# Down-projection weight sums made during the up stage and streamed, in a float32 transformer layer on one core

## The chip, the core and the metric

The kernel runs on one core of a Trainium2 chip. The metric is the device time of one launch in microseconds. Five engines work side by side: TensorE (PE in the profile, PEld its weight loads), VectorE (DVE), ScalarE (ACT), GpSimd (POOL), and SyncE (SP), which here only issues DMAs. Each engine runs its own list of instructions in order and waits on semaphores for the others. TensorE's clock is granted in two levels, 2.4 GHz (1.00 in the profile) and 1.2 GHz (0.5).

## The reference

One layer of a generator over 2048 tokens of width 1024. Only its second half matters here:

```
h2 = modulate(rmsnorm(x, norm2_g), shift, scale)
gate, up = split(h2 @ w_up, 2)               # w_up: 1024 x 5632, so 2816 columns each
gate = depthwise_conv(gate, conv_w, conv_b)  # 3 taps along the tokens
x = x + mod * ((silu(gate) * up) @ w_down)   # w_down: 2816 x 1024
return rmsnorm(x, final_norm_g)              # all float32
```

The 2816 hidden channels are 22 blocks of 128, in two halves of 11.

## The kernel before

The first 1060 us (modulation, first projection, the three head groups and the output projection) are not touched. Then comes the feed-forward part, in two stages.

**Float32 by three matmuls.** Every operand is split by `halves` into a high half (copied by ACT, line 1100) and a low half (a subtraction on DVE or POOL, line 1101; the fifth argument says which). A product of two split operands is three matmuls: high by high, high by low, low by high.

**One level of Winograd's scheme.** Both matrix products are cut in 2 by 2 blocks and done with seven products of block sums in place of eight: B11, T2, T1, T3, B21, T4, B22, numbered 0 to 6 in the names. So the operands are sums of blocks: T1 uses a21+a22 of the weights, T2 that less a11, B22 a12 less that, T3 a11-a21.

**Up stage.** Tokens go in two halves, t = 0 and 1. For each t there are eleven pairs k: one `winograd` for the gate (names `g_k`) and one for the up half (`u_k`), each 84 matmuls of 128x512 on line 1290. DVE empties the PSUM banks x, y, z (lines 1301 to 1312), ACT starts the convolution (line 1341) and DVE does its other two taps (line 1343), POOL makes the sums of the next weights and of the results, and POOL's DMA queue stores the results to DRAM (`actd`). The generator `second_half`, advanced by `step`, prepares the second token half during t = 0. During t = 1 `step` does nothing.

**Down stage.** For each t seven `product`s in the order B11, B21, T2, T1, T3, B22, T4, each of 11 k with 12 matmuls of 128x512 (line 1487) into four PSUM banks (named p, pu or pv). The activations come back from `actd` in tiles `ra` of two k; their halves are `ah`. `w_down` (four blocks, 11.5 MB) is loaded to SBUF once, in pieces, over the first products, and stays. `down_weight` makes the sums for T2, T1, T3 and B22 again for each t, on POOL (names `dw..s`, lines 1447 to 1451), for B22 partly on DVE (1451, 1453), and its halves are `dw..hl` (the digits are t, product and k). POOL also does the low halves of `ra` for B11, B21, T4 and every second one of B22: 72 in all.

After a product, `adds` adds its banks to the residual tile `x1r` (line 1501), squares what is final on ACT (1504), adds up the squares on DVE (1508), and `finish` makes the statistics: one matmul against ones (1513), square root (1519), reciprocal (1520) and eight scalings (1526, 1524), with the stores of the output.

**What sets the order.** The program is written in one stream; a scheduler orders each engine's list by a simulated timeline when it is built, under the limits of the tile pools (a tag with `bufs=n` is a ring of n buffers; a new tile waits for the readers of the one it replaces). Loads go through SP's queue, stores of the up stage through POOL's. On the chip each list is strictly in order.

Of the kernel before, what the change touches and what calls it, by code (L numbers as in the profile page):

```python
# [18 lines left out]
P = 128  # L19
# [14 lines left out]
TB = 512  # L34
# [109 lines left out]
def tile_hybrid_block(ctx: ExitStack, tc: tile.TileContext, a, out):  # L144
# [41 lines left out]
          for p in range(7)]  # L186
    actd = [[dp.tile([P, NP, TB], F32, name=f"actd{t}{p}") for p in range(7)] for t in range(2)]
# [1094 lines left out]
    last_up = [None]  # L1282
# [11 lines left out]
    def winograd(w, c12, c21, c22, use_c11, name, step):  # L1294
# [10 lines left out]
        nc.vector.tensor_tensor(c22, c22, z, op=ALU.add)  # L1305
# [9 lines left out]
    def up_pair(t, k, wg, wu):  # L1315
        nm = f"{t}_{k}"

        def step():
            if t == 0 and k > 0:
                next(sh, None)  # L1320
# [15 lines left out]
        for i, l in ((0, 0), (1, 1), (1, 0), (0, 1)):  # L1336
# [3 lines left out]
            ps = c if t else pp.tile([P, TB], F32, tag="st", bufs=1, name=f"cs{nm}{i}{l}")  # L1340
# [42 lines left out]
    sh = second_half()  # L1383
    for t in range(2):
# [14 lines left out]
    with ExitStack() as down:  # L1399
# [4 lines left out]
        dn, dx, da, dw0, dpad, dwh, dw1, dah, dw2 = (pool(f"dn{i}") for i in range(9))  # L1404
        dpad.tile([P, 2048], F32, name="dpad")
# [3 lines left out]
        CH = ((0, 4), (4, 8), (8, NP))  # L1409
        wq = {}  # L1410

        def wd_tiles(i, j, pool):
            wq[i, j] = [pool.tile([P, b - a_, TB], F32, name=f"wd{i}{j}{a_}") for a_, b in CH]

        def wd_load(i, j, c):
            load(wq[i, j][c], a["w_down"][i, j][:, CH[c][0]:CH[c][1], :])

        def x1_tile(t, l, fo):
            return dx.tile([P, TB], F32, tag="x1", bufs=16, name=f"x1r{t}{l}{fo}")
# [6 lines left out]
        X1_ORDER = [(l, 4 * i + m) for i, l in ((0, 0), (0, 1), (1, 1), (1, 0)) for m in range(4)]  # L1426
        wd_tiles(0, 1, dw0)
        wd_tiles(1, 0, dw0)
        wd_tiles(0, 0, dw1)
        wd_tiles(1, 1, dw2)  # L1430
        x1s = [{lf: x1_tile(0, *lf) for lf in X1_ORDER}, {}]
        for c in range(3):
            wd_load(0, 0, c)
        none = [(lambda: None, ())]
        x1_loads = [(x1_load, (0,) + lf) for lf in X1_ORDER]
        ahead = iter(none * 10 + [(wd_load, (0, 1, 0))] + none * 3
                     + x1_loads[:4] + [(wd_load, (0, 1, 1)), (wd_load, (0, 1, 2))] + x1_loads[4:]
                     + [(wd_load, (1, j, c)) for c in range(3) for j in range(2)])

        def down_weight(p, k, name):  # L1440
            a11, a12, a21, a22 = (wq[i, j][k // 4][:, k % 4, :] for i in range(2) for j in range(2))
            if p in (B11, B21, T4):
                src = {B11: a11, B21: a12, T4: a22}[p]
            else:
                src = dn.tile([P, TB], F32, tag="ws", bufs=3, name=name + "s")
                if p == T3:
                    nc.gpsimd.tensor_tensor(src, a11, a21, op=ALU.subtract)
                else:
                    nc.gpsimd.tensor_tensor(src, a21, a22, op=ALU.add)
                    if p != T1:  # L1450
                        (nc.vector if p == B22 else nc.gpsimd).tensor_tensor(src, src, a11, op=ALU.subtract)
                        if p == B22:
                            nc.vector.tensor_tensor(src, a12, src, op=ALU.subtract)
# [188 lines left out]
```

## Time and profile before

| | |
|---|---|
| median of 3 runs | 2392.19 us (2389.84 to 2395.36) |
| the profiled execution | 2384.91 us, span 2382.9 us |
| PE busy | 2268.9 us, 95% |
| DVE busy | 1818.5 us, 76% |
| POOL busy | 1045.1 us, 44% |
| down stage, first to last matmul | 1903.0 to 2364.7 us |

The profile is one execution. Busy times are sums over the instructions of an engine; a wait of DVE for its operands' port inside an instruction counts as busy. A row of the timeline is one instruction, or several alike in a row (the xN at its end), and the bracket behind it says how long the engine stood idle before it and what released it.

### The profile page before, as it was taken

The numbers are of one execution on the slowest core, as the hardware profiler recorded it, in microseconds if no ns is written. First come the engines' busy times: TensorE is split into PE (matmuls) and PEld (weight loads), VectorE is DVE, ScalarE is ACT, GpSimd is POOL, SyncE is SP. The second block draws the span as 40 slices with busy tenths as digits, with TensorE's granted clock in tenths as the row PEclk, the third lists the DMA queues.
The fourth block names the chain that finished last, engine by engine and source line by source line (L and its number), as shares of the span: only waits on it lengthen the run. The fifth ranks groups of instructions, "written<-read, shape, count | busy, mean of one in ns | idle before, by whom it ended". The sixth has DMA issues, their size and how long they took to land.

```text
span 2382.9 us, 34374 instructions
## 1 busy us (share of the span) xinstructions
PE 2268.9 (95%) x12452; PEld 1890.4 (79%) x12452; DVE 1818.5 (76%) x2503; ACT 1140.8 (48%) x2018; POOL 1045.1 (44%) x982
## 2 busy tenths in 40 slices
PE   7999989999999899999999999999999999989996
PEld 5889768988888688878787887788888887768875
DVE  4786656556785884796899977687787889988997
ACT  4764643357455446554444534344343444344442
POOL 0265312111012122225656665556556477665763
PEclk9999999999999999999999999999999999999998
DMA  9775576657878778643344435433333482245322
GB/s 352 241 243 181 197 238 189 184 171 230 247 223 274 204 211 298 225 160 104 142 162 174 162 130 204 162 103 111 101 107 106 157 334 89 80 150 165 96 81 92
DMA packets 179226, 421.70 MB, mean 177 GB/s; under 512 B 19952, under 2 KB 68976, under 8 KB 177008
## 3 DMA queue, kind: packets, MB, share of 16 engines
q1 hardware_dynamic: 144688, 318.82, 42.5%
q0 software_dynamic: 28320, 94.39, 10.6%
q10 hardware_dynamic: 6048, 6.29, 0.8%
q8 instruction: 98, 1.61, 0.3%
q14 instruction: 72, 0.59, 0.1%
HBM read 311.69 MB, written 107.74 MB: 176 GB/s over the span
## 4 chain that ended last, share of the span: by engine, by line
PE 51%; DVE 21%; DMA 12%; issue 8%; ACT 4%; POOL 3%; SPq 1%; DVEq 0%; ACTq 0%; POOLq 0%
DVE cv L573 3%; PE po L202 3%; PE obank L202 3%; PE pu L1487 2%; PE p L1487 2%; PE pq L202 2%; PE s L202 2%; PE tp L208 2%; DVE ah L1101 2%; PE pk L202 2%; PE tp L202 2%; PE pv L1487 2%; DMA bias_t<-in_bias 1%; DMA kk<-ks 1%; POOL ah L1101 1%
## 5 line engine op out<-in xcount | busy, mean ns | idle before, releaser
L573 DVE SCALAR_TENSOR_TENSOR cv<-hconv,cst,cv 128x512 f32<-128x512 f32 x240 | 214.5, 935 | 10.8 <-ACT cv L567 10.6
L693 DVE CUSTOM_DVE_ANT_0 sb<-s,bias_t 128x544 f32<-128x544 f32 (+3 forms) x128 | 105.1, 821 | 105.7 <-PE s L202 73.8
L696 ACT ACTIVATE sb<-sb,mx 128x544 f32<-128x544 f32 (+3 forms) x128 | 106.3, 831 | 161.5 <-DVE mx L693 158.6
L1101 POOL TENSOR_TENSOR ah<-ra,ah 128x512 fp32r<-128x512 f32 x72 | 110.5, 1548 | 79.0 <-ACT ah L1100 79.0
L1100 ACT ACTIVATE ah<-ra 128x512 fp32r<-128x512 f32 x154 | 95.0, 622 | 93.5 <-PE p L1487 28.6
L202 PE MATMUL s<-kk,qq 128*128 128x256 f32 (+4 forms) x512 | 102.8, 323 | 14.9 <-DVE mx L693 7.5
L202 PEld LDWEIGHTS s<-kk,qq 128*128 128x128 f32 x512 | 88.4, 191 | 34.7 <-DVE mx L693 13.7
L208 PE MATMUL tp<-cst,sb 128*128 128x128 f32 (+2 forms) x672 | 97.9, 276 | 12.9 <-DVE pt L728 9.1
L208 PEld LDWEIGHTS tp<-cst,sb 128*128 128x128 f32 (+2 forms) x672 | 80.0, 139 | 32.4 <-DVE pt L728 10.6
L1345 ACT ACTIVATE c<-c 128x512 f32<-128x512 f32 x88 | 55.4, 630 | 100.8 <-DVE c L1343 100.6
L1343 DVE SCALAR_TENSOR_TENSOR c<-gb,cst,c 128x512 f32<-128x512 f32 x88 | 97.5, 1131 | 1.5 <-ACT c L1341 1.3
L1101 DVE TENSOR_TENSOR ah<-ra,ah 128x512 fp32r<-128x512 f32 x82 | 83.9, 1028 | 12.4 <-ACT ah L1100 12.4
L196 POOL DMA_DIRECT2D x1d<-x x30 | 16.4, 548 | 143.1 <-DVE x L859 109.8
L966 POOL TENSOR_TENSOR adaf<-adaf,adaf 128x1024 f32<-128x1024 f32 x16 | 41.1, 2568 | 84.4 <-ACT adaf L963 84.4
L726 ACT ACTIVATE pt<-tp 128x384 f32<-128x384 f32 (+2 forms) x128 | 61.0, 477 | 35.5 <-PE tp L208 35.1
L728 DVE COPY pt<-tp 128x256 f32<-128x256 f32 (+1 forms) x128 | 57.6, 450 | 23.4 <-PE tp L208 23.0
L963 ACT ACTIVATE adaf<-adaf,silu_c 128x256 f32<-128x256 f32 x128 | 54.2, 497 | 43.8 <-DMA adaf<-in_ada 40.0
L196 POOL DMA_DIRECT2D ks<-k x60 | 33.4, 559 | 78.7 <-ACT k L226 48.6
L196 POOL DMA_DIRECT2D mixd<-att x14 | 7.7, 554 | 134.1 <-DVE att L227 130.2
L196 POOL DMA_DIRECT2D actd<-c x66 | 36.6, 554 | 65.2 <-DVE c L1353 47.9
L202 PE MATMUL obank<-pt,vt 128*64 128x128 f32 (+2 forms) x832 | 58.4, 277 | 0.2 <-DVE pt L728 0.2
L1353 DVE TENSOR_TENSOR c<-c,u 128x512 f32<-128x512 f32 x66 | 52.1, 790 | 0.5
(2411 smaller groups left out, 8015.5 us busy)
## 6 DMA issues: line engine op xcount, KB each, us to landing
ra<-actd SPq DMA_DIRECT2D x70, 512.0 KB
wg<-in_w_up SPq DMA_DIRECT2D x44, 512.0 KB
wu<-in_w_up SPq DMA_DIRECT2D x44, 512.0 KB
actd<-tt POOLq DMA_DIRECT2D x88, 256.0 KB, 2.4
actd<-c POOLq DMA_DIRECT2D x66, 256.0 KB, 2.3
adaf<-in_ada SPq DMA_DIRECT2D x32, 512.0 KB
qq<-qs SPq DMA_DIRECT2D x64, 256.0 KB
adaf<-in_ada SPq DMA_DIRECT2D x8, 1024.0 KB
```

The costliest lines, as they stand in the source:

```text
L196: st_eng[0].dma_start(plain(dst), plain(src))
L202: x = nc.tensor.matmul(*args, **kw)
L208: x = nc.tensor.transpose(*args)
L573: nc.vector.scalar_tensor_tensor(acc[ct], hb[:, ct, k:k + TB], cvw[:, ct, k:k + 1], acc[ct], op0=ALU.mult, op1=ALU.add)
L693: x = nc.vector.tensor_tensor_reduce(out=sb[:, w], in0=s[:, w], in1=bt[:, w], scale=-1.0, scalar=3.0e38, op0=ALU.add, op1=ALU.min, accum_o ...
L696: nc.scalar.activation(sb[:, w], sb[:, w], AF.Exp, bias=mx, scale=-1.0, accum_out=rs[:, cb, j:j + 1])
L726: nc.scalar.activation(dst, src, AF.Copy)
L728: nc.vector.tensor_copy(dst, src)
L1100: nc.scalar.activation(hl[:, 0, :], src, AF.Copy)
L1101: eng.tensor_tensor(hl[:, 1, :], src, hl[:, 0, :].bitcast(F32), op=ALU.subtract)
L1343: nc.vector.scalar_tensor_tensor(to, gb[:, i, o + d:o + d + TB], fcw[:, f, d:d + 1], ps, op0=ALU.mult, op1=ALU.add)
L1487: nc.tensor.matmul(ps[i], w[:, ww, sl], ah[:, aa, :], start=start and k_ == 0 and m == 0, stop=(k_ == NP - 1 and m == 2), skip_group_check ...
```

## The change

1. `down_sums`, a generator advanced by `step` in the pairs k >= 2 of t = 1, loads `w_down` once more, in 22 pieces of 512 KB (ring `sp` of 3), makes the four sums with 4 DVE additions per k (44 in all) in place, and stores them with 22 stores of 512 KB through POOL's queue to two DRAM tensors `sd`.
2. In t = 1 (but not for k = 10) the first convolution tap is written to a PSUM bank, as it was in t = 0 already.
3. In the down stage no sums are made. Each product loads its own weights, two k at a time, from `w_down` or `sd` (tiles `wd`, ring of 4). The ring of `ra` has 3 buffers, before 4; `ah` has two rings of 4, before one of 6. All 32 tiles of the residual are loaded early. POOL does the low halves of the activations for B21 alone (22), DVE all others. The halves of the first six k of the first product are issued after the last addition of c22 of the up stage.
4. The last statistics (t = 1, first half of the tokens) take the last square unsummed, as a second matmul into the same bank, in columns: 8 matmuls of one column, square root and reciprocal on 128x4, 4 matmuls that spread the result, and one ACT copy for POOL; DVE reads it from PSUM.

The matmuls of the products are the same in number, kind and order. Line numbers shift: 1101 becomes 1103, 1304 to 1310 become 1324 to 1330, 1353 becomes 1375, 1501 and 1508 become 1495 and 1504. Over the whole program POOL's tensor_tensor instructions go from 533 to 373 and its DMAs from 328 to 350, DVE's tensor_tensor from 1239 to 1288, and SP's weight loads for the down stage from 12 to 84, beside the 22 of `down_sums`.

```diff
+    sd = [dp.tile([P, NP, 2, TB], F32, name=f"sd{j}") for j in range(2)]
+    def down_sums():
+        yield
+        for k in range(NP):
+            x, y = (fws.tile([P, 2, TB], F32R, tag="sp", bufs=3, name=f"wds{k}{j}").bitcast(F32) for j in range(2))
+            for j, q in ((0, x), (1, y)):
+                with tc.issue_after(last_w[0]):
+                    load(q, a["w_down"][:, j, :, k, :].rearrange("i p c -> p i c"))
+            a11, a21, a12, a22 = x[:, 0, :], x[:, 1, :], y[:, 0, :], y[:, 1, :]
+            nc.vector.tensor_tensor(a22, a21, a22, op=ALU.add)
+            nc.vector.tensor_tensor(a21, a11, a21, op=ALU.subtract)
+            yield
+            nc.vector.tensor_tensor(a11, a22, a11, op=ALU.subtract)
+            nc.vector.tensor_tensor(a12, a12, a11, op=ALU.subtract)
+            for j, q in ((0, x), (1, y)):
+                store(sd[j][:, k], q)
+            yield
...
-            if t == 0 and k > 0:
+            if t and k > 1:
+                next(dw, None)
+            elif not t and k > 0:
                 next(sh, None)
...
-            ps = c if t else pp.tile([P, TB], F32, tag="st", bufs=1, name=f"cs{nm}{i}{l}")
+            ps = c if t and k == NP - 1 else pp.tile([P, TB], F32, tag="st", bufs=1, name=f"cs{nm}{i}{l}")
...
+        DOWN_W = {B11: a["w_down"][0, 0], B21: a["w_down"][0, 1], T4: a["w_down"][1, 1],
+                  T2: sd[0][:, :, 0, :], T3: sd[0][:, :, 1, :], B22: sd[1][:, :, 0, :], T1: sd[1][:, :, 1, :]}
...
-                        at = da.tile([P, 2, TB], F32, tag="ra", bufs=4, name=f"ra{t}{p}{k}")
+                        wt = dwd.tile([P, 2, TB], F32, tag="wd", bufs=4, name=f"wd{t}{p}{k}")
+                        load(wt[:, 0:n, :], DOWN_W[p][:, k:k + n, :])
+                        at = da.tile([P, 2, TB], F32, tag="ra", bufs=3, name=f"ra{t}{p}{k}")
                         last_ra[0] = load(at[:, 0:n, :], actd[t][p][:, k:k + n, :])
...
-                    ah = halves(at[:, k % 2, :], dah, "ahl", 6, f"ah{t}{p}{k}",
-                                nc.gpsimd if p in (B11, B21, T4) and (t or p or k > 3) or p == B22 and k % 2 else nc.vector)
+                    order = tc.issue_after(last_c22[0]) if (t, p) == (0, B11) and k < 6 else nullcontext()
+                    with order:
+                        ah = halves(at[:, k % 2, :], (dah, dai)[k % 2], "ahl", 4, f"ah{t}{p}{k}",
+                                    nc.gpsimd if p == B21 else nc.vector)
+                        wh = halves(wt[:, k % 2, :], dwh, "whl", 6, f"dw{t}{p}{k}", nc.vector)
...
-                    ops.append((k, down_weight(p, k, f"dw{t}{p}{k}"), ah))
+                    ops.append((k, wh, ah))
...
+                if last:
+                    sq = acc[l], acc["last"]
+                    for i in range(4):
+                        for j, x in enumerate(sq):
+                            mm(ps[:, i:i + 1], x[:, i * P:(i + 1) * P], ones_d[:, 0:1], start=j == 0, stop=j == 1)
...
+                    col = cp.tile([P, 4], F32, tag="col", bufs=2, name=f"frs{t}{l}")
+                    nc.scalar.activation(col, ps[:, 0:4], AF.Sqrt, bias=eps)
+                    nc.vector.reciprocal(col, col)
+                    pr = dnp.tile([P, TB], F32, tag="y", name="fmr")
+                    for i in range(4):
+                        mm(pr[:, i * P:(i + 1) * P], col[:, i:i + 1].to_broadcast([P, P]), ident, start=True, stop=True)
+                    r = dn.tile([P, TB], F32, tag="rstd", bufs=1, name="frs")
+                    nc.scalar.activation(r, pr, AF.Copy)
```

How the change moves DVE's list is shown at three places; in a row stand the line, the operation, what is written and what is read. The first is in pair 3 of t = 1, around the drains of the gate's banks (`g1_3y`, `g1_3z`). Before:

```order
L1305 TENSOR_TENSOR gb_10781<-gb_10781,g1_3z_15386 128x512
L1101 TENSOR_TENSOR wu1_3hl3_15501<-wu1_3s2_15486,wu1_3hl3_15501 128x512
L1343 SCALAR_TENSOR_TENSOR c1_300_15513<-gb_10781,cst_75,c1_300_15513 128x512
L1310 TENSOR_TENSOR gb_10781<-g1_3p1_15387,g1_3y_15385 128x512
L1101 TENSOR_TENSOR wu1_3hl4_15504<-wu1_30_15480,wu1_3hl4_15504 128x512
L1343 SCALAR_TENSOR_TENSOR c1_311_15518<-gb_10781,cst_75,c1_311_15518 128x512
```

Now, where `wds40` and `wds41` are the two tiles of `down_sums` for k = 4:

```order
L1325 TENSOR_TENSOR gb_10783<-gb_10783,g1_3z_15416 128x512
L1270 TENSOR_TENSOR wds41_15835<-wds40_15834,wds41_15835 128x512
L1103 TENSOR_TENSOR wu1_3hl3_15541<-wu1_3s2_15526,wu1_3hl3_15541 128x512
L1365 SCALAR_TENSOR_TENSOR cs1_300_15554<-gb_10783,cst_75,cs1_300_15554 128x512
L1271 TENSOR_TENSOR wds40_15834<-wds40_15834 128x512
L1103 TENSOR_TENSOR wg1_4hl0_15714<-wg1_40_15702,wg1_4hl0_15714 128x512
L1273 TENSOR_TENSOR wds40_15834<-wds41_15835,wds40_15834 128x512
L1274 TENSOR_TENSOR wds41_15835<-wds41_15835,wds40_15834 128x512
L1330 TENSOR_TENSOR gb_10783<-g1_3p1_15417,g1_3y_15415 128x512
```

The four additions stand between the last addition of c22 (1325, before 1305) and the drain for c21 (1330, before 1310), where two weight halves and a convolution tap stood; this repeats once per winograd.

The second place is the end of the up stage, DVE's last drains of the winograd `u1_10` and the first halves of the down stage (`dw00..` weights, `ah00..` activations of product B11, t = 0). Before:

```order
L1304 TENSOR_TENSOR u_10780<-u1_10p1_17615,u1_10y_17613 128x512
L1376 TENSOR_TENSOR pc_83<-ue_82,pc_83 128x11
L1101 TENSOR_TENSOR dw000hl_17828<-wd000_17794,dw000hl_17828 128x512
L1305 TENSOR_TENSOR u_10780<-u_10780,u1_10z_17614 128x512
L1101 TENSOR_TENSOR dw001hl_17846<-wd000_17794,dw001hl_17846 128x512
L1101 TENSOR_TENSOR dw002hl_17866<-wd000_17794,dw002hl_17866 128x512
L1353 TENSOR_TENSOR c1_1011_17597<-c1_1011_17597,u_10780 128x512
L1101 TENSOR_TENSOR dw003hl_17884<-wd000_17794,dw003hl_17884 128x512
L1101 TENSOR_TENSOR dw004hl_17904<-wd004_17795,dw004hl_17904 128x512
L1101 TENSOR_TENSOR dw005hl_17923<-wd004_17795,dw005hl_17923 128x512
L1310 TENSOR_TENSOR u_10780<-u1_10p1_17615,u1_10y_17613 128x512
```

Now:

```order
L1325 TENSOR_TENSOR u_10782<-u_10782,u1_10z_17766 128x512
L1103 TENSOR_TENSOR dw000_17987<-wd000_17980,dw000_17987 128x512
...
L1103 TENSOR_TENSOR ah005_18088<-ra004_18066,ah005_18088 128x512
L1103 TENSOR_TENSOR dw005_18091<-wd004_18064,dw005_18091 128x512
L1103 TENSOR_TENSOR ah002_18024<-ra002_18022,ah002_18024 128x512
L1375 TENSOR_TENSOR c1_1011_17749<-c1_1011_17749,u_10782 128x512
L1103 TENSOR_TENSOR ah004_18068<-ra004_18066,ah004_18068 128x512
L1330 TENSOR_TENSOR u_10782<-u1_10p1_17767,u1_10y_17765 128x512
```

Between the addition of c22 (1325) and the next drain (1330) there are now twelve low halves, eleven ahead of the product c1_1011 and one behind it (seven are left out above), where there were five; the weight halves `dw000` that stood ahead of 1305 are behind it.

The third is in the down stage, product B22 of t = 0 (`dw06..`, `ah06..`). Before, with the sums `dw06..s` between the halves:

```order
L1453 TENSOR_TENSOR dw066s_19206<-wd014_17789,dw066s_19206 128x512
L1451 TENSOR_TENSOR dw067s_19228<-dw067s_19228,wd004_17795 128x512
L1451 TENSOR_TENSOR dw068s_19253<-dw068s_19253,wd008_17796 128x512
L1453 TENSOR_TENSOR dw067s_19228<-wd014_17789,dw067s_19228 128x512
L1101 TENSOR_TENSOR dw066hl_19210<-dw066s_19206,dw066hl_19210 128x512
L1453 TENSOR_TENSOR dw068s_19253<-wd018_17790,dw068s_19253 128x512
L1101 TENSOR_TENSOR ah068_19250<-ra068_19247,ah068_19250 128x512
L1101 TENSOR_TENSOR dw067hl_19232<-dw067s_19228,dw067hl_19232 128x512
L1101 TENSOR_TENSOR dw068hl_19257<-dw068s_19253,dw068hl_19257 128x512
L1451 TENSOR_TENSOR dw069s_19263<-dw069s_19263,wd008_17796 128x512
L1453 TENSOR_TENSOR dw069s_19263<-wd018_17790,dw069s_19263 128x512
L1451 TENSOR_TENSOR dw0610s_19276<-dw0610s_19276,wd008_17796 128x512
```

Now:

```order
L1103 TENSOR_TENSOR dw065_19314<-wd064_19288,dw065_19314 128x512
L1103 TENSOR_TENSOR ah066_19334<-ra066_19331,ah066_19334 128x512
L1504 TENSOR_TENSOR sq014_19192<-sq014_19192,sq017_19203 128x512
L1103 TENSOR_TENSOR dw066_19337<-wd066_19329,dw066_19337 128x512
L1103 TENSOR_TENSOR ah068_19375<-ra068_19372,ah068_19375 128x512
L1103 TENSOR_TENSOR dw067_19355<-wd066_19329,dw067_19355 128x512
L1103 TENSOR_TENSOR ah069_19381<-ra068_19372,ah069_19381 128x512
L1103 TENSOR_TENSOR dw068_19378<-wd068_19370,dw068_19378 128x512
L1103 TENSOR_TENSOR ah0610_19392<-ra0610_19389,ah0610_19392 128x512
L1103 TENSOR_TENSOR dw069_19384<-wd068_19370,dw069_19384 128x512
L1103 TENSOR_TENSOR ah051_19494<-ra050_19473,ah051_19494 128x512
L1103 TENSOR_TENSOR dw0610_19395<-wd0610_19387,dw0610_19395 128x512
```

The sums (1451, 1453) are gone, and in their place stand the low halves of the activations with odd k, which POOL made before, each ahead of the weight halves of the k before it.

## Rows read from the trace of the kernel before

**Rows 1.** The page, engines over the whole span: busy us (share) x instructions.

```profile
PE 2268.9 (95%) x12452; PEld 1890.4 (79%) x12452; DVE 1818.5 (76%) x2503; ACT 1140.8 (48%) x2018; POOL 1045.1 (44%) x982
```

**Rows 2.** Windows: from:to, length, busy (instructions) per engine, PEclk, DMA share, GB/s.

```profile
1903.00:2365.00 462.00, 437.76 (x1855) 352.90 (x1853) 421.68 (x411) 194.52 (x365) 293.08 (x191) 0.97 0.41 138
2079.00:2086.00 7.00, 6.05 (x14) 4.79 (x15) 6.96 (x8) 1.87 (x4) 4.80 (x3) 0.51 0.12 49
```

**Rows 3.** Timeline of PE, down stage: start, duration, engine, line, operation, count.

```profile
1903.01 2.88 PE L1487 MATMUL p<-ah,dw000hl 128*128 128x512 f32 x12
1905.73 2.88 PE L1487 MATMUL p<-ah,dw001hl 128*128 128x512 f32 x12
...
2364.05 0.84 PE L1487 MATMUL pu<-ah,dw1510hl 128*128 128x512 f32 x3
```

**Rows 4.** Waits of PE, down stage: waiter, releaser, us in total, times, longest.

```profile
PE fms L1513 <- DVE sq L1508: 7.4, 2, 5.4
PE pv L1487 <- ACT dw066hl L1100: 1.7, 1, 1.7
...
PE pv L1487 <- DVE ah L1101: 0.3, 1, 0.3
```

**Rows 5.** Groups by line, down stage: count, busy us, mean ns, idle before.

```profile
L1101 POOL TENSOR_TENSOR ah<-ra,ah 128x512 fp32r<-128x512 f32 x72 | 110.5, 1548 | 79.0 <-ACT ah L1100 79.0
L1101 DVE TENSOR_TENSOR ah<-ra,ah 128x512 fp32r<-128x512 f32 x82 | 83.9, 1028 | 12.4 <-ACT ah L1100 12.4
```

**Rows 6.** Line 1101, down stage: ns shortest/median/longest, first and last start.

```profile
L1101 DVE TENSOR_TENSOR ah<-ra,ah x82: 673/684/1785, 1902.7 to 2321.2; 128x512 fp32r<-128x512 f32 x82
```

**Rows 7.** Windows: six pairs of t = 0, then three of t = 1.

```profile
1130.00:1370.00 240.00, 231.54 (x1003) 189.90 (x1003) 215.98 (x262) 108.19 (x181) 153.39 (x184) 0.99 0.46 161
1591.00:1705.00 114.00, 114.00 (x505) 94.41 (x504) 90.37 (x111) 46.89 (x77) 66.09 (x66) 1.00 0.31 105
```

**Rows 8.** Waits of PE, up stage of t = 0.

```profile
PE g_2y L1290 <- DVE gb L1304: 3.4, 1, 3.4
```

**Rows 9.** Groups, DVE's convolution taps: in t = 1, then in t = 0.

```profile
L1343 DVE SCALAR_TENSOR_TENSOR c<-gb,cst,c 128x512 f32<-128x512 f32 x80 | 91.7, 1170 | 1.5 <-ACT c L1341 1.3
...
L1343 DVE SCALAR_TENSOR_TENSOR cs<-gb,cst,cs 128x512 f32<-128x512 f32 x37 | 27.7, 749 | 8.7 <-ACT cs L1341 8.4
```

**Rows 10.** Stores of 512 KB by POOL's queue (`td` from `tbs`, 16): issue to landing.

```profile
DMA to landing us min/median/max: 2.9/2.9/5.3
```

**Rows 11.** Timeline of DVE, end of the up stage.

```profile
1897.90 0.68 DVE L1305 TENSOR_TENSOR u<-u,u_10z 128x512 f32<-128x512 f32 x1
1898.50 0.69 DVE L1101 TENSOR_TENSOR dw001hl<-wd,dw001hl 128x512 fp32r<-128x512 f32 x1
...
1902.11 0.68 DVE L1310 TENSOR_TENSOR u<-u_10p,u_10y 128x512 f32<-128x512 f32 x1
```

**Rows 12.** Windows: heaviest load traffic of the down stage.

```profile
1920.00:1925.00 5.00, 5.00 (x24) 4.13 (x23) 5.00 (x1) 1.91 (x5) 4.98 (x5) 1.00 1.04 406
```

**Rows 13.** Timeline of all engines, behind the last product.

```profile
2366.45 0.69 DVE L1508 TENSOR_TENSOR sq<-sq,sq 128x512 f32<-128x512 f32 x1 [0.76 <-ACT sq L1504]
...
2367.20 1.13 PE L1513 MATMUL fms<-sq,cst 128*128 128x512 f32 x2 [2.31 <-DVE sq L1508]
...
2369.08 3.35 DVE L1520 RECIPROCAL frs<-frs 128x512 f32<-128x512 f32 x1 [1.94 <-ACT frs L1519]
2372.47 6.51 DVE L1526 SCALAR_TENSOR_TENSOR x1r<-x1r,cst,frs 128x512 f32<-128x512 f32 x5
2372.51 4.59 POOL L1524 TENSOR_TENSOR x1r<-x1r,frs 128x512 f32<-128x512 f32 x3 [21.57 <-DVE frs L1520]
```

**Rows 14.** Column statistics of an earlier norm: ns shortest/median/longest, first and last start.

```profile
L202 PE MATMUL n2last<-cst,ssum_last x8: 164/250/251, 1106.2 to 1106.9; 128*128 128x1 f32 x8
L202 PE MATMUL n2last<-cst,n2lastc x8: 272/275/276, 1112.3 to 1113.1; 128*128 128x128 f32 x8
L318 DVE RECIPROCAL n2lastc<-n2lastc x1: 177/177/177, 1108.7 to 1108.7; 128x4 f32<-128x4 f32 x1
```

More of the change, by code (lines that the diff above doesn't have):

```diff
@@ L1304, in winograd @@
         nc.vector.tensor_tensor(c22, p1, y, op=ALU.add)
-        nc.vector.tensor_tensor(c22, c22, z, op=ALU.add)
+        last_c22[0] = nc.vector.tensor_tensor(c22, c22, z, op=ALU.add).ins
         step()
@@ L1390, in tile_hybrid_block @@
             reload()
+    run_all(dw)
     last_column()
@@ L1401, in pool @@
             return down.enter_context(tc.tile_pool(name=name, bufs=1, reuse_waits="tile"))
-        dn, dx, da, dw0, dpad, dwh, dw1, dah, dw2 = (pool(f"dn{i}") for i in range(9))
-        dpad.tile([P, 2048], F32, name="dpad")
+        dn, dxa = pool("dn0"), pool("dn1")
+        dpa = pool("dpa")
+        dpa.tile([P, 3080], F32, name="dpa")
+        da, dxb, dpb = pool("dn2"), pool("dn3"), pool("dpb")
+        dpb.tile([P, 4344], F32, name="dpb")
+        dah, dwd, dwh, dai = (pool(f"dn{i}") for i in range(4, 8))
         dnp = Banks(tc, "dn", (("y", 4), ("x", 4)))
@@ L1408, in tile_hybrid_block @@
         LAST = 3
[L1409 to L1419, printed above, removed]
         last_ra = [None]
+        X1_ORDER = [(l, 4 * i + m) for i, l in ((0, 0), (0, 1), (1, 1), (1, 0)) for m in range(4)]
@@ L1423, in x1_load @@
+        x1s = [{(l, fo): (dxb if t else dxa).tile([P, TB], F32, tag="x1", bufs=16, name=f"x1r{t}{l}{fo}")
+                for l, fo in X1_ORDER} for t in range(2)]
         def x1_load(t, l, fo):
             load(x1s[t][l, fo], x1d[2 * t + l, :, fo, :])
[L1426 to L1453, printed above, removed]
-            return halves(src, dwh, "whl", 6, name + "hl", nc.vector)
@@ L1456, in tile_hybrid_block @@
+        ahead = iter([(lambda: None, ())] * 4 + [(x1_load, (t,) + lf) for t in range(2) for lf in X1_ORDER])
+        DOWN_W = {B11: a["w_down"][0, 0], B21: a["w_down"][0, 1], T4: a["w_down"][1, 1],
+                  T2: sd[0][:, :, 0, :], T3: sd[0][:, :, 1, :], B22: sd[1][:, :, 0, :], T1: sd[1][:, :, 1, :]}
         for t in range(2):
             x1 = x1s[t]
-            if t == 1:
-                for l, fo in X1_ORDER:
-                    x1[l, fo] = x1_tile(t, l, fo)
-                ahead = iter([(x1_load, (t,) + lf) for lf in X1_ORDER])
@@ L1506, in adds @@
                             acc[l] = sq
+                        elif t == 1 and l == 0 and i == 1 and m == 3:
+                            acc["last"] = sq
                         else:
@@ L1511, in finish @@
             def finish(l):
[L1512 to L1513 removed]
                 last = t == 1 and l == 0
                 pool_ = range(1, KT, 3) if last else ()
[L1516 to L1520 removed]
+                ps = dnp.tile([P, TB], F32, tag="y", name=f"fms{t}{l}")
+                if last:
[3 more added lines that the diff above has]
+                            mm(ps[:, i:i + 1], x[:, i * P:(i + 1) * P], ones_d[:, 0:1], start=j == 0, stop=j == 1)
+                    for fo in pool_:
+                        nc.scalar.activation(x1[l, fo], x1[l, fo], AF.Copy, scale=fng[:, fo:fo + 1])
+                    col = cp.tile([P, 4], F32, tag="col", bufs=2, name=f"frs{t}{l}")
[6 more added lines that the diff above has]
+                    nc.scalar.activation(r, pr, AF.Copy)
+                else:
+                    mm(ps, ones_d, acc[l], start=True, stop=True)
+                    r = pr = dn.tile([P, TB], F32, tag="rstd", bufs=1, name=f"frs{t}{l}")
+                    nc.scalar.activation(r, ps, AF.Sqrt, bias=eps)
+                    nc.vector.reciprocal(r, r)
                 for fo in range(KT):
```

19 lines of the change are left out of this document (6 added, 13 removed).

## The prediction

> **What bounds the kernel now.** I read the busy times first: PE works 95% of the span [rows 1], so time can only be won where PE waits or runs at its lower clock. Then the windows and PE's timeline stage by stage. In three pairs of t = 1 in the up stage PE is busy 114.00 of 114.00 us [rows 7]: nothing can be won there, only lost. In the down stage it is busy 437.76 of 462 us [rows 2], and the timeline gives the loss exactly. Undisturbed, twelve matmuls take 1905.73 - 1903.01 = 2.72 us [rows 3], so 2.72 x 11 x 14 products = 418.9 us. The stage runs from 1903.01 to 2364.05 + 0.68 (three matmuls of 0.227) = 2364.7, which is 461.7 us. **42.8 us are lost between products' first and last matmul.**
>
> What the loss is made of: the waits of PE there are 18 kinds, the first 7.4 us for the two statistics matmuls `fms`, whose squares DVE adds up late, and the others, from 1.7 down to 0.3 us, for halves made by DVE and ACT, all but one of weights [rows 4]. They are DVE's lateness: it is busy 421.68 of 462 us [rows 2]. That is not its work, though, but its price: the same subtraction takes 684 ns at its median and up to 1785 [rows 6], 1028 on the mean, while POOL is busy 293 us [rows 2] with its own subtractions of 1548 ns [rows 5] and the sums. A wait costs twice: after one in B22 the granted clock is 0.51, that is 1.2 GHz, in the window from 2079 to 2086 [rows 2].
>
> **The waits in the down stage.** The change takes from POOL its 110 weight sums of this stage (for each t and k one for T1, one for T3, one for B22, two for T2) and 50 of its 72 low halves, so that it is idle but for product B21. DVE loses its 44 sums of B22 and gets the 50 low halves. At the pitch without POOL beside it, 1898.50 - 1897.90 = 0.60 us [rows 11], the heaviest product (T4 with the end of B22's statistics) has 22 low halves = 13.2 us, 4 additions of banks and 4 of squares = 5.5, a reciprocal of 3.35 [rows 13] and 8 scalings of 0.7 = 5.6: 27.7 of the 29.92 us of a product. It fits, and DVE can run ahead into the lighter products before it. The squares for `fms` then have no slow neighbour: the chain from the last matmul of B22 is four additions and four squares' additions in step with ACT, some 4.5 us, and PE comes to `fms` only behind the first k of T4, some 10 us after that matmul. So its 7.4 us go too. What stays is the work of the `fms` matmuls, three in the stage, 1.13 us each [rows 13] = 3.4, and I leave 2 for a start of B21, where POOL still subtracts beside DVE. Gain: 42.8 - 5.4 = **37.4 us**. Bounds: 42.8 if nothing stays, 20 if about half of the waits turn out to be ACT's and not DVE's.
>
> **Streamed weights and activations.** Each product now brings 2.88 MB of weights beside 2.88 MB of activations in 29.9 us, 193 GB/s; in the first two products the residual's 8.4 MB come too, 19.9 MB, of which some 3.5 MB are loaded before: 16.4 MB in 60 us, 274 GB/s. The core has moved 406 GB/s here, with the DMA engines full [rows 12]. The rings give a load the time of four to five k, 10.9 to 13.6 us, against 2.9 to 5.3 us from issue to landing for 512 KB, as the stores of that size show [rows 10]. Cost: nothing; its cover is that lead. If it were gone, PE would wait at each of the 77 pairs of k.
>
> **The sums in the up stage.** Added in six pairs (k = 2 to 7) are 44 DVE additions, 22 loads and 22 stores. Taken away is the slow form of the convolution: 1170 ns per tap from SBUF against 749 through PSUM [rows 9], 8 taps a pair, 3.4 us. DVE has 90.37/3 = 30.1 us of work in a 38 us pair [rows 7]; 44/6 = 7.3 additions at the mean of the down stage, 1028 ns [rows 5], make 7.5. So 30.1 - 3.4 + 7.5 = 34.2 of 38, 90%. In six pairs of t = 0, where DVE carries a second task in just this way, it is also at 90% (215.98 of 240), and there PE loses 240 - 231.54 = 8.5 us [rows 7], mostly in waits for a bank that DVE empties, of 3.4 us at the longest [rows 8]. That is the nearest row. POOL has less to do in t = 1 (0.58 of the time against 0.64), so I take **+6 us**, bounds 0 and +20.
>
> The Trainium skill, page "SBUF — State Buffer", section "SBUF: two separate sides", says that a DVE instruction with two SBUF operands and a GpSimd instruction that reads SBUF exclude each other for the whole of an instruction. The longest and shortest of one form, 1785 and 673 ns [rows 6], agree, and the rule speaks against these additions, which have two SBUF operands beside a POOL that works over half the time. If every one met a POOL instruction, DVE would have 30.1 - 3.4 + 7.3 x 1.785 = 39.7 us of work in a 38 us pair, some +10 us over six pairs.
>
> **The end of the up stage.** Before, the drain on line 1310 of the last winograd started at 1902.11, with five low halves between it and the addition of c22 at 1897.90 [rows 11]. Now twelve low halves and a product stand there, and ACT must make the twelve high halves ahead of them, none earlier than c22's end. The addition and thirteen more instructions of 0.60 bring that drain's start to 1897.90 + 14 x 0.60 = 1906.3 and its end to 1906.9, or 1907.5 if ACT sets the pace. The third bank of the first down product is one that it empties; PE reaches it after half of the first k, at 1903.01 + 1.36 = 1904.4. Queued behind PE's wait is the whole down stage. **+3 us**, bounds 0 (if the list is caught up) and +5.
>
> **The end.** Behind the last product stands a chain: sum of squares to 2367.1, matmul 1.13, square root, a reciprocal of 3.35, five scalings in 6.51 beside three of POOL in 4.59 [rows 13]. In columns the matmuls take 0.7 to 1.0 us for eight, the reciprocal 0.18, the spread 0.8 to 1.1 [rows 14]: from the last square to the first scaling some 3.3 us in place of 6.0. The scalings read the factor from PSUM and need not share with POOL, but POOL's three of 1.5 stay, behind a copy, so that most of this gain is not at the end: **-4 us**, bounds -2 and -6.
>
> **The sum.** +6 + 3 - 37.4 - 4 = -32.4 us. Against the profiled execution of 2384.9 that is 2352.5; the median of the runs lies 7.3 us above that execution, and I put the same difference there: 2392.2 - 32.4 = **2360 us**.
>
> **The rivals.**
>
> *The up stage pays more.* The 44 additions stand between DVE's drains of c22 and c21, so a late one makes PE wait for a bank. For it: that PE has no slack of its own there (114.00 of 114.00), and the three waits of t = 0. Against it: DVE's share comes out no higher than in t = 0. Once a pair at 3.4 us [rows 8] makes 6 x 3.4 = 20.4 in place of 6: 2392.2 - 38.4 + 20.4 = 2374.
>
> *The streamed loads come late.* For it: the ring of activations is shorter, every load is in one queue, in order, behind loads that wait for their buffers. Against it: 193 GB/s of 406. At half a microsecond per pair of k, 77 x 0.5 = 38.5: 2360 + 38.5 = 2398.5, nothing won. A miss of 0.1 us would cost 7.7.
>
> *Slower: the chain of the sums through DRAM buffers.* The ring of the sums has three tiles for two per k, so the second tile of k + 1 can be loaded only when the first of k is stored. From DVE's last addition of k through POOL's turn (up to 1.6), the store, the load (in SP's list, with the up weights behind it) to DVE's first addition of k + 1 there are about 14 us, counted by the places in the winograds of 19 us. The chain costs 1.2 + 1.6 + 2.9 + 2.9 = 8.6 us by the median landing and 13.4 by the longest [rows 10]. It fits by both; if POOL gets to its stores later, DVE stands still in front of the drain for c21 and PE with it, eleven times. From 3.5 us each it eats the 38.4 won elsewhere; at 4 it is 2392.2 - 38.4 + 44 = 2398.
>
> **Chances.** My forecast 0.66; the up stage paying more 0.20; both of these are faster. The streamed loads late 0.05, of which 0.03 slower and 0.02 no change; the chain through DRAM 0.06, slower; the rest 0.03, of which 0.02 no change and 0.01 slower. A measurement of this kernel can tell 0.2% (5 us) from no change. So faster 0.86, the same 0.04, slower 0.10. The range: the low end has the waits all gone, the up stage free and the tail at its best, -42.8 - 6 + 3 = -46, so 2346; the high end takes in the up stage's +20 and some of the lost waits staying, 2381. The forecast's own range is 2349 to 2371.
>
> **What would show it.** In the profile after: twelve matmuls each 2.72 us through nearly all fourteen products, and the down stage about 424 us long; no wait of `fms` for squares; DVE's low halves near 0.68 us outside B21, and DVE far under 90% busy there. In pairs 2 to 7 of t = 1 PE busy about 97%, with waits for drains; PE's wait in the first k of the down stage between 2 and 4 us. Wrong would be: PE waiting for weight loads; a down stage over 440 us, so that the waits were not POOL's doing; PE idle 20 us or more in pairs 2 to 7.

## The result and the profile after

The changed kernel takes 2364.7 us (median of 4 runs, 2359.99 to 2366.42) against 2391.0 us before: 26.3 us less, ratio 0.9884, 95% interval 0.9864 to 0.9904. The forecast was 2360, with a range of 2346 to 2381. The profiled execution is 2365.5 us with a span of 2363.7.

The page, in the columns of [rows 1], shows that PE's work is the same and that DVE and POOL have 108 and 251 us less:

```profile
PE 2268.4 (96%) x12474; PEld 1898.5 (80%) x12474; DVE 1710.7 (72%) x2552; ACT 1138.6 (48%) x2019; POOL 793.8 (34%) x844
```

The windows after answer to [rows 2 and 7]; the first is the down stage, the second the stretch of t = 1 that holds all additions of the sums:

```profile
1923.00:2349.00 426.00, 423.56 (x1856) 349.02 (x1854) 289.89 (x417) 194.98 (x363) 41.95 (x32) 1.00 0.64 219
1530.00:1760.00 230.00, 220.66 (x960) 180.23 (x958) 200.18 (x251) 86.83 (x146) 134.44 (x151) 0.99 0.55 199
```

The down stage took 461.7 us and takes 425.9; PE is idle in it for 2.4 us, at its start. DVE fell from 421.68 to 289.89 us, though it has six instructions more (411 to 417). In the second window PE loses 9.3 us; before the change it lost 0.1 in the same one (229.93 of 230).

All waits of PE from the first down product on, after, in the columns of [rows 4]: none is for a half or a load, and none of the long ones for `fms` is left.

```profile
PE p L1481 <- DVE u L1330: 2.4, 1, 2.4
PE fms L204 <- ACT sq L1498: 1.0, 1, 1.0
PE fmr L204 <- DVE frs L1521: 0.6, 1, 0.6
PE fms L204 <- DVE sq L1504: 0.2, 1, 0.2
```

In PE's timeline the second down stretch starts behind the wait for the drain on line 1330, 14 matmuls at 0.36 us in place of 0.227: the clock is slow behind the wait, with a granted 0.66 on the mean from 1927 to 1932 us and 1.00 in the 5 us after. The first product takes 34.3 us, the others 29.92, or 30.83 with a matmul `fms` in them.

```profile
1923.17 1.52 PE L1481 MATMUL p<-ah,dw 128*128 128x512 f32 x6
1927.14 5.07 PE L1481 MATMUL p<-ah,dw 128*128 128x512 f32 x14 [2.44 <-DVE u L1330]
```

DVE's timeline there answers to [rows 11]: from the addition of c22 to the drain are 8.43 us, before 4.21.

```profile
1917.98 0.68 DVE L1325 TENSOR_TENSOR u<-u,u_10z 128x512 f32<-128x512 f32 x1
1918.58 0.68 DVE L1103 TENSOR_TENSOR dw<-wd,dw 128x512 fp32r<-128x512 f32 x1
...
1926.41 0.68 DVE L1330 TENSOR_TENSOR u<-u_10p,u_10y 128x512 f32<-128x512 f32 x1
```

In t = 1 of the up stage DVE itself waits, in the waits of DVE from 1475 to 1920 us (total, times, longest), for the loads of the sums. That DVE stands still for such a load in front of a drain I had only as a rival:

```profile
DVE wds L1270 <- DMA wds<-in_w_down: 15.8, 7, 4.5
```

The timelines around one of these waits show POOL's stores, then SP's loads, then DVE:

```profile
1656.00 0.56 POOL L198 DMA_DIRECT2D sd<-wds  x1 [2.11 <-DVE wds L1273]
...
1658.46 0.54 POOL L198 DMA_DIRECT2D sd<-wds  x1 [1.34 <-DVE wds L1274]
```

```profile
1657.62 2.71 SPq L195 DMA_DIRECT2D wg<-in_w_up  x2
1660.43 2.03 SPq L195 DMA_DIRECT2D wds<-in_w_down  x2
```

```profile
1662.90 0.74 DVE L1365 SCALAR_TENSOR_TENSOR cs<-gb,cst,cs 128x512 f32<-128x512 f32 x1
1668.17 3.08 DVE L1270 TENSOR_TENSOR wds<-wds,wds 128x512 f32<-128x512 f32 x1 [4.53 <-DMA wds<-in_w_down]
1671.18 0.67 DVE L1324 TENSOR_TENSOR gb<-g_4p,g_4y 128x512 f32<-128x512 f32 x1
```

The load stands in SP's list behind two loads of up weights, is issued at 1660.43 and is there at 1668.17. DVE stood still in front of it since 1663.6, then took 3.08 us for one addition, and the drain on 1324 behind it made PE wait 2.6 us. (Here the first addition stands ahead of both drains for c22: the order shown for pair 3 does not hold for every winograd.) The ring of the sums is not what held the load: the store from 1656.00 had landed at 1658.89. It is the list. The change ties these loads to the load of the last up weights (`issue_after(last_w[0])`), and SP waited for the buffers of those two loads until DVE had made the halves that read them:

```profile
SPq L195 <- DVE wg_4hl L1103: 16.6, 2, 14.6
```

The waits of PE make up the 9.3 us that it lost in the second window, and not all of them come from loads:

```profile
PE g_1z L1310 <- DVE gb L1325: 3.0, 1, 3.0
PE g_4y L1310 <- DVE gb L1324: 2.6, 1, 2.6
PE g_5y L1310 <- DVE gb L1324: 2.0, 1, 2.0
PE u_3x L1310 <- ACT u_3p L1319: 1.3, 1, 1.3
PE u_6x L1310 <- DVE wu_6hl L1103: 0.4, 1, 0.4
```

Late loads stand in front of `g_4y` and `g_5y`, 4.6 us. In front of the longest, `g_1z`, stands one low half on DVE that took 5.47 us, while POOL went from one instruction to the next (1551.86 to 1557.44):

```profile
1552.53 5.47 DVE L1103 TENSOR_TENSOR wu_1hl<-wu,wu_1hl 128x512 fp32r<-128x512 f32 x1
```

In the two profiles of before, no half of DVE in t = 1 took more than 2.37 us. Behind the wait of `g_1z` the granted clock was 0.5 for 3.4 us, that is 1.2 GHz.

The end, in the columns of [rows 13]: from the last matmul (2349.1) to the end of the span are 14.6 us, before 18.2. The scalings read PSUM and take 3.38 us in place of 6.51.

```profile
2352.91 0.18 DVE L1521 RECIPROCAL frs<-frs 128x4 f32<-128x4 f32 x1 [2.83 <-ACT frs L1520]
...
2353.15 1.46 PE L204 MATMUL fmr<-cst,frs 128*128 128x128 f32 x8 [0.57 <-DVE frs L1521]
...
2355.27 3.38 DVE L1537 SCALAR_TENSOR_TENSOR x1r<-x1r,cst,fmr 128x512 f32<-128x512 f32 x5 [2.18 <-ACT frs L1526]
2355.32 3.71 POOL L1535 TENSOR_TENSOR x1r<-x1r,frs 128x512 f32<-128x512 f32 x3 [173.84 <-ACT frs L1526]
```

### The profile page after: what moved, and what is told of

It reads as the page before. It is cut to its first block, busy times and chain, and to the rows that moved or that the text cites. A ratio compares the mean times of both kernels' runs of the same rounds, so it can differ in the third digit from the quotient of the medians.

```text
span 2363.7 us, 34634 instructions
## 1 busy us (share of the span) xinstructions
PE 2268.4 (96%) x12474; PEld 1898.5 (80%) x12474; DVE 1710.7 (72%) x2552; ACT 1138.6 (48%) x2019; POOL 793.8 (34%) x844
## 4 chain that ended last, share of the span: by engine, by line
PE 52%; DVE 15%; issue 13%; DMA 12%; ACT 4%; POOL 2%; SPq 1%; POOLq 0%; DVEq 0%; ACTq 0%
PE po L204 4%; PE p L1481 4%; PE pu L1481 4%; PE obank L204 3%; PE pk L204 3%; DMA adaf<-in_ada 3%; PE pv L1481 3%; PE s L204 2%; PE tp L210 2%; PE tp L204 2%; PE pq L204 2%; DMA wds<-in_w_down 2%; SPq L195 1%; DVE cv L575 1%; PE tg L204 1%
## 5 line engine op out<-in xcount | busy, mean ns | idle before, releaser
L1103 DVE TENSOR_TENSOR dw<-wd,dw 128x512 fp32r<-128x512 f32 x154 | 114.1, 749 | 103.3 <-ACT dw L1102 100.8
L1481 PE MATMUL pu<-ah,dw 128*128 128x512 f32 x792 | 181.7, 390 | 0.0
L1481 PEld LDWEIGHTS pu<-ah,dw 128*128 128x128 f32 x792 | 148.7, 188 | 31.8 <-issue 1.0
L1102 ACT ACTIVATE dw<-wd 128x512 fp32r<-128x512 f32 x154 | 96.0, 628 | 159.7 <-PE pu L1481 58.3
L1481 PE MATMUL p<-ah,dw 128*128 128x512 f32 x528 | 122.5, 394 | 2.4 <-DVE u L1330 2.4
L1481 PE MATMUL pv<-ah,dw 128*128 128x512 f32 x528 | 120.3, 389 | 0.0
L1481 PEld LDWEIGHTS p<-ah,dw 128*128 128x128 f32 x528 | 100.2, 190 | 24.3 <-DVE u L1330 2.9
L1481 PEld LDWEIGHTS pv<-ah,dw 128*128 128x128 f32 x528 | 99.1, 188 | 20.6
L210 PEld LDWEIGHTS tp<-cst,sb 128*128 128x128 f32 (+2 forms) x672 | 79.9, 138 | 31.6 <-DVE pt L730 9.9
L1103 POOL TENSOR_TENSOR ah<-ra,ah 128x512 fp32r<-128x512 f32 x22 | 32.9, 1510 | 210.2 <-ACT ah L1102 208.8
L1365 DVE SCALAR_TENSOR_TENSOR cs<-gb,cst,cs 128x512 f32<-128x512 f32 x84 | 62.9, 749 | 21.9 <-ACT cs L1363 21.6
```

Source lines behind the costliest of these rows:

```text
L210: x = nc.tensor.transpose(*args)
L1102: nc.scalar.activation(hl[:, 0, :], src, AF.Copy)
L1103: eng.tensor_tensor(hl[:, 1, :], src, hl[:, 0, :].bitcast(F32), op=ALU.subtract)
L1365: nc.vector.scalar_tensor_tensor(to, gb[:, i, o + d:o + d + TB], fcw[:, f, d:d + 1], ps, op0=ALU.mult, op1=ALU.add)
L1481: nc.tensor.matmul(ps[i], w[:, ww, sl], ah[:, aa, :], start=start and k_ == 0 and m == 0, stop=(k_ == NP - 1 and m == 2), skip_group_check ...
```

## The experiments

One table for all, read from PE's timeline in one profile of each run: "t = 1" is from the first matmul of that half (`g_0x`) to the first of the down stage, "down" from there to the end of its last. Theories A and B are those of the expectation above each result. Six of the profiles have the same up stage (after, the four runs that put work back into the down stage, statistics as before); their t = 1 lies between 448.5 and 449.9 us.

| run | median us | t = 1 | first product | down |
|---|---|---|---|---|
| before (two profiles) | 2391.0 | 438.3, 434.7 | 29.9 | 461.7, 462.0 |
| after | 2364.7 | 449.1 | 34.3 | 425.9 |
| additions on POOL | 2379.6 | 449.6 | 34.3 | 441.8 |
| halves on POOL | 2364.1 | 448.6 | 34.7 | 426.4 |
| halves on POOL, additions on DVE | 2368.8 | 449.9 | 35.9 | 429.4 |
| all three | 2422.3 | 449.4 | 34.6 | 482.9 |
| sums by rows | 2359.3 | 450.3 | 33.8 | 425.5 |
| sums gated | 2358.9 | 444.2 | 32.2 | 423.9 |
| start of the down stage | 2362.7 | 451.0 | 29.9 | 421.6 |
| first tap in SBUF | 2363.7 | 449.5 | 32.3 | 424.4 |
| statistics as before | 2368.3 | 448.5 | 34.3 | 425.9 |
| gated + start | 2355.6 | 445.2 | 29.9 | 421.6 |
| gated + start + spread | 2346.4 | 435.6 | 29.9 | 421.6 |

**What made the halves late.** First POOL's additions alone:

```diff
+                    for j in range({T2: 2, T1: 1, T3: 1, B22: 1}.get(p, 0)):
+                        nc.gpsimd.tensor_tensor(pad[:, j * TB:(j + 1) * TB], wt[:, k % 2, :], at[:, k % 2, :], op=ALU.add)
```

> The changed kernel with 110 additions put back on POOL in the down stage, where the sums were: two per k in T2, one in T1, T3 and B22, reading the loaded weight and activation tiles and writing a scratch tile that nobody reads. No result depends on them. Theory A, POOL beside DVE is what made the halves late: the low halves on DVE outside B21 go from 0.70 us to about 1.0, PE waits for halves come back, and the down stage goes from 426 us to 436 or more, the time up by 10 to 25 us. Theory B, what counted was the chain through POOL's sums and DVE's 44 sums, and the neighbour as such costs nothing: the stage stays at 426 to 429 us and the time within 3 us.

Measured: 441.8 us for the stage, +15 us in the time (2379.6). The groups of DVE's low halves from 1930 to 2345 us, in the columns of [rows 5], and the window:

```profile
L1103 DVE TENSOR_TENSOR dw<-wd,dw 128x512 fp32r<-128x512 f32 x146 | 152.7, 1054 | 43.5 <-ACT dw L1102 43.4
L1103 DVE TENSOR_TENSOR ah<-ra,ah 128x512 fp32r<-128x512 f32 x124 | 136.9, 1105 | 1.9 <-ACT ah L1102 1.9
```

```profile
1930.00:2345.00 415.00, 404.92 (x1757) 330.35 (x1756) 363.47 (x389) 186.97 (x355) 226.27 (x140) 0.99 0.63 214
```

In the changed kernel these halves take 0.752 and 0.702 us on the mean, and DVE is busy for 279.17 us of this window. So 84 us more for DVE come from additions of another engine whose results nothing waits for. PE loses only in T2, 12.6 us in t = 0 and 3.0 in t = 1, the product with two additions per k: theory A, but in one product of four. There DVE is full, in T2 of t = 0 for 41.87 of 42.50 us:

```profile
1986.20:2028.70 42.50, 34.37 (x133) 26.02 (x132) 41.87 (x33) 15.29 (x34) 38.47 (x24) 0.92 0.50 153
```

Then the halves, back on POOL as before:

```diff
-                                    nc.gpsimd if p == B21 else nc.vector)
+                                    nc.gpsimd if p in (B11, B21, T4) and (t or p or k > 3) or p == B22 and k % 2 else nc.vector)
```

> The changed kernel with the low halves of the activations shared out as before the change (72 on POOL: B11 but its first k, B21, T4, every second one of B22), and the sums still made in the up stage. Theory A (the neighbour costs): the products B22 and T4 lose again, the stage goes to 430 to 445 us, the time up by 4 to 20 us. Theory B (the work costs): DVE has 50 instructions less, POOL is fast enough without the sums, and the stage stays at 424 to 428 us.

Measured: 426.4 us for the stage, the time the same. POOL's 50 more halves bring DVE's weight halves to 0.887 us on the mean, and cost PE nothing, since DVE has 50 instructions less (275.70 us busy). Theory B here: this part of the change brings nothing by itself.

With 44 additions on DVE in B22 as well (two lines as above, on `nc.vector`, `if p == B22`):

> The changed kernel with POOL's 72 low halves as before the change and 44 additions on DVE put back in product B22 (two per k), where its sums were, reading loaded tiles and writing a scratch tile that nobody reads. POOL makes no additions. In the run with 110 additions on POOL only T2 lost, 12.6 and 3.0 us, so B22's and T4's losses of before are not explained by those. Theory A, they were DVE's own additions: B22 and T4 lose together 10 us or more over both t, the stage is 436 us or more, and squares for fms come late. Theory B, it takes DVE's additions and POOL's at the same time: the stage stays at 426 to 430 us.

Measured: 429.4 us, of which `fms` waits 1.8 for squares. DVE is busy 307.91 of 415 us. Theory B.

All three together:

> The changed kernel with all three put back as loads of the engines, without the chain between them: POOL's 72 low halves, its 110 additions and DVE's 44. The additions' results are not used. Theory A, load and neighbour together made the 42.8 us lost before: the stage goes to 450 to 465 us, T2, B22 and T4 losing as they did, the time to 2385 to 2400 us. Theory B, the chain (a half must wait for the sum that POOL makes) made a good part of it: the stage stays under 445 us.

Measured: 482.9 us for the stage, 57 more than the changed kernel, where the change itself had saved 35.8; stage and time (2422.3) lie above what either theory expected. The waits of PE:

```profile
PE pu L1485 <- DVE dw L1103: 15.0, 10, 3.0
PE pv L1485 <- DVE dw L1103: 11.8, 5, 5.4
PE fms L204 <- DVE sq L1508: 5.4, 2, 4.0
PE pv L1485 <- ACT dw L1102: 3.5, 1, 3.5
```

They are of the kinds of [rows 4]. T2, B22 and T4 lose 12.3, 23.5 and 8.9 us over both t (over 29.92 us, 30.83 where an `fms` stands), before 7.4, 19.4 and 11.9; T3 loses 11.9 too, which it did not before; that the additions don't stand at the old places of the lists may be why, but is not shown. So losses of this size need no chain from sum to half, which speaks for theory A. But the run is no copy of the loss before. The additions read the loaded tiles, whose buffers can't be loaded again before that, and loads of `ra` come late: ACT waits for them 79.9 us on line 1462, against 29.0 in the changed kernel and 49.7 (line 1472) before.

```profile
ACT ra L1462 <- DMA ra<-actd: 79.9, 25, 10.9
```

The windows of B22, t = 0, in this run and before the change, differ in DVE:

```profile
2094.50:2133.30 38.80, 33.23 (x133) 26.17 (x132) 30.47 (x37) 15.36 (x33) 18.06 (x12) 0.91 0.54 175
2059.10:2101.00 41.90, 35.95 (x133) 27.46 (x132) 39.88 (x41) 16.06 (x33) 29.39 (x18) 0.88 0.20 58
```

In this run DVE is idle for 8.3 of the 38.8 us, so not all of the loss is DVE's time. Before the change it was idle for 2.0 of 41.9, so there neither a chain nor a load held it for long. Its 41 instructions at 0.68 us each [rows 6] would take 27.9 us, an estimate, and fit into a product's 29.92: in B22 of before the price shows in the trace itself. What T4 lost beside its wait for squares is not separated. And the parts don't add: 15.8 us for POOL's additions, 0.4 for the halves, 3.0 for DVE's additions on top of these, 57 for all.

**Where the up stage lost.** The tiles by rows, the first addition's tile one k ahead:

```diff
-                    load(q, a["w_down"][:, j, :, k, :].rearrange("i p c -> p i c"))
+            x, y = ahead_, row(k, 0)
+            if k + 1 < NP:
+                ahead_ = row(k + 1, 1)
```

> The changed kernel with the tiles of the sums in the up stage cut by rows in place of columns, and the tile that the first addition reads loaded one k ahead; the same bytes, additions and buffers. Theory A, PE's waits in pairs 2 to 6 come from loads that land late in front of DVE's drains: DVE's wait for these loads goes from 15.8 us to under 4, t = 1 of the up stage gets 4 to 7 us shorter, and so does the time. Theory B, they come from DVE's additions running beside POOL: the wait for loads goes, and PE's waits stay, the time within 2 us.

Measured: t = 1 takes 450.3 us. The wait only moved to the second addition, which needs the tile that is still late:

```profile
DVE wds L1277 <- DMA wds<-in_w_down: 22.5, 10, 4.3
```

It tells nothing between the theories. Nor does the time: the median is 2359.3, but the runs lie between 2357.9 and 2367.5, and the profiled one is the slowest. The next run takes the wait away:

```diff
+            with tc.issue_after(last_c22[0]):
+                nc.vector.tensor_tensor(a22, a21, a22, op=ALU.add)
+                nc.vector.tensor_tensor(a21, a11, a21, op=ALU.subtract)
```

> The changed kernel with each first pair of additions of the sums issued after the addition of c22 of its own winograd; the scheduler had put them one winograd ahead, right behind their loads. So the loads, which are issued as before, have more time to land. The run with tiles cut by rows moved DVE's wait for loads to its second addition (22.5 us in all), and PE's waits stayed. Theory A, late loads in front of DVE's drains make PE's waits: DVE's wait for these loads falls under 4 us and t = 1 of the up stage, 449 us from its first matmul to the down stage, gets 4 to 7 us shorter. Theory B, DVE's additions beside POOL make them: t = 1 stays within 2 us of 449.

Measured: 444.2 us for t = 1, 4.9 less. The median is 5.8 us less (2358.9), with runs from 2350.9 to 2361.7 that overlap those of the changed kernel. DVE's wait for these loads:

```profile
DVE wds L1271 <- DMA wds<-in_w_down: 2.6, 2, 1.9
```

Theory A, by what it expected, and for nearly half of the loss. The gate does a second thing, though: it takes the additions away from in front of the drains for c22, and PE's wait in `g_1z`, which no load had made, is gone too. So the 4.9 us are not the price of late loads alone. The first tap in SBUF again (`ps = c if t`):

> The changed kernel with the first tap of the convolution in t = 1 in SBUF again, as before the change; the sums stay. Theory A, DVE's work beside POOL in the pairs that carry the sums counts: 48 taps there at 1.17 us in place of 0.74 are 3.4 us more of DVE's time a pair, and t = 1 of the up stage (449 us from its first matmul to the down stage) gets 8 to 30 us longer, the time too. Theory B, only the late loads count there: t = 1 is within 4 us of 449.

Measured: 449.5 us for t = 1, the time the same (2363.7). The taps of t = 1 take 944 ns on the mean, against 749 and 740 through PSUM, and not the 1170 that the expectation counted with. Theory B: the tap's move to PSUM pays nothing here.

**The start and the end.**

```diff
-                    order = tc.issue_after(last_c22[0]) if (t, p) == (0, B11) and k < 6 else nullcontext()
+                    order = tc.issue_after((last_c21 if k > 1 else last_c22)[0]) if (t, p) == (0, B11) and k < 6 else nullcontext()
```

> The changed kernel with the halves of k = 2 to 5 of the first down product issued after the last drain of c21 in place of the last addition of c22, so that this drain stands behind four low halves and not twelve. Theory A: PE's wait of 2.4 us for that drain and the slow clock behind it go, the first product takes 30 us in place of 34.3, the time is 3 to 4.5 us less. Theory B: the wait moves to the halves of k = 1 to 3, which now come later, and the time is within 1.5 us.

Measured: the first product takes 29.92 us, 4.3 less: theory A for the stage. The medians differ by 2.0 us, less than the spread of the runs. One group of 38 matmuls without a wait, in PE's timeline:

```profile
1921.40 8.78 PE L1481 MATMUL p<-ah,dw 128*128 128x512 f32 x38
```

The statistics as before (`if False` for `if last`):

> The changed kernel with the last statistics as before: the last square added on DVE, one matmul of 512 columns, a reciprocal of 128x512, and scalings that read the factor from SBUF. My step: from the last matmul of the products to the end takes 18.2 us as before, in place of 14.6, and the time is 3.6 us more. Rival, the end hangs on the output's DMAs: the same 14.6 within 1 us.

Measured: 18.9 us from the last matmul to the end in place of 14.6: my step. The median is 3.6 us more (2368.3, runs from 2365.2 to 2372.7, which overlap those of the changed kernel).

**The part that neither kernel changed.**

> The kernel before, unchanged, for a second profile. Up to the second half of the up stage both kernels have the same instructions in the same order, but the profile after reaches that point 9.3 us later (1474.1 against 1464.8 us). Theory A, executions differ by that much there: this profile starts the second half between 1467 and 1475 us. Theory B, something in the changed kernel (its tensors in DRAM, its tiles) slows the part before: this profile starts it within 2 us of 1464.8.

Measured: it starts t = 1 at 1473.3 us. Theory A: the first profile of before was quick up to there (1464.8; the other thirteen profiles lie between 1466.8 and 1475.4). So the profiles' difference, 19.4 us, is 7 to 9 us too small, and the medians' 26.3 stands.

**Both edits, and the sums spread.**

> The changed kernel with the additions of the sums issued after c22 of their own winograd and the halves of k = 2 to 5 of the first down product issued after the drain of c21, the two edits that each shortened its stage. If the two are separate, t = 1 takes about 444 us, the first product 29.9 us, and the time is 5 to 9 us under the changed kernel's 2364.7. If the gain of one was the other's (or chance), 0 to 4 us.

Measured: 445.2 and 29.9 us, 2355.6 (2350.9 to 2356.8): 9.1 us under the changed kernel, both gains in one.

```diff
-            if t and k > 1:
+            if t and k > 1 and (2 * k + up_half[0]) % 3 != 2:
                 next(dw, None)
```

> As the run with both edits, and the sums spread over the pairs 2 to 10 in place of 2 to 7, by leaving out every third winograd. If what is left of t = 1's loss (444 against 435 to 438 us before the change) is DVE's load in the pairs with sums, it falls by 2 to 5 us more; if it is the additions standing in front of a drain, as many as before, it stays within 1.5 us.

Measured: t = 1 takes 435.6 us, as before the change and 9.6 less than with both edits, more than either case expected; and the time is 2346.4 us (2344.95 to 2349.32): ratio to before 0.9809, interval 0.9795 to 0.9824. DVE has no wait for a load of the sums. The window of before:

```profile
1530.00:1760.00 230.00, 229.65 (x1011) 189.34 (x1011) 202.37 (x248) 92.29 (x154) 132.70 (x148) 1.00 0.48 167
```

PE loses 0.35 us while DVE is busy 202.37 us, where the changed kernel lost 9.3 at 200.18: DVE's mean load in this stretch doesn't tell the loss. That fewer sums stand in it, or that there is a winograd without any to catch up in, this run doesn't separate. It is 45.9 us under the kernel before and 18.3 under the changed one.

## Why the prediction was right, and where not

- **Waits in the down stage, forecast -37.4.** Without the start of the first product, the 14 products lost 42.8 us and lose 2.7, all in the three `fms` matmuls: -40.1. Right in size, and in the reason as far as it is shown: DVE's price beside POOL makes the loss in T2 (the run with POOL's additions) and in B22 (the trace of before); for the rest it is argued. What I did not see is that this price counts only where it brings DVE's time near the product's. The low halves moved off POOL paid nothing alone.
- **Streamed loads, forecast 0.** Right: PE waited for none, at 219 GB/s in the stage. The price of the rival was counted with 77 loads of weights; six per product make 84.
- **Sums in the up stage, forecast +6.** The weakest step: 10.8 us against the first profile of before, 14.4 against the second. I compared DVE's shares with those of t = 0 and counted the way of a tile as 14 us by its places, with the up weights behind the loads of the sums. They stand ahead of them, by the change's own `issue_after`, and the scheduler put the additions right behind their loads. So what the chain rival feared, DVE standing still in front of a drain, was at work inside my likeliest case, with 15.8 us of DVE's waiting, though by another link than the ring. Beside it stood what I had priced only by a mean, one half of 5.47 us in front of a drain. The gate takes back 3.9 to 4.9 us (two profiles), gate and spreading together 13.5.
- **The rule on the shared port.** In the run with additions on POOL nothing but the neighbour was added, and DVE's halves went from 0.70 and 0.75 us to 1.11 and 1.05. The Trainium skill, page "SBUF — State Buffer", section "SBUF: two separate sides", has a DVE instruction with two SBUF operands and a GpSimd instruction that reads SBUF block each other, and this run agrees. The +10 us that the prediction worked out beside this rule for the up stage are near the 10.8 measured, but partly by luck: 4.6 of PE's 9.3 us of waits stand behind late loads, and one blocked half makes 3.0.
- **The first tap through PSUM.** I took 3.4 us of DVE a pair for it; its loss would have cost nothing.
- **End of the up stage, forecast +3.** 2.4 us of wait and 1.9 of slow clock behind it, 4.3 in all; the run that moves the halves gives all of it back.
- **The end, forecast -4.** -3.6.
- **The sum, forecast -32.4.** By stages +10.8 to +14.4, +4.3, -40.1 and -3.6 make -28.6 to -25.0; the medians say -26.3. That the sum came out within 6.1 us is in part luck: the down stage gained 2.7 us more than forecast while the up stage lost 4.8 to 8.4 more.

## What to carry to other kernels

Work that takes two engines' time on the same memory has a price that is seen in the other engine's durations; compare the shortest and the mean of one form before counting instructions, but expect time from removing it only where the slowed engine has no slack left. When work is moved into a stage where TensorE has no idle time, its mean load says little: look at what stands behind each moved instruction in its list, and at the list that its loads stand in. A scheduler that places work right behind a simulated load gives it no lead; tie it to a later event, and give the engine room between such places.

## What was not expected of the hardware

- Two loads of 512 KB issued together behind two of up weights, with stores under way, took 7.7 us from the first one's issue to the addition that needs them (1660.43 to 1668.17), against 2.9 for one store in [rows 10]; the DMA engines were busy 0.98 and 0.80 of the two windows of 4 us between.
- Single additions on DVE beside POOL took up to 3.33 us (`wds`, line 1270, x11: 680 ns at the shortest, 1360 at the median), where the mean that I had counted with was 1.03. The low half of 5.47 us is longer still.
